# A transformer block on one core: feed-forward in two phases, attention beside recurrence, seven block products in place of eight

## The chip, the core and the metric

The kernel runs on one of the eight cores of one Trainium2 chip. The metric is the device time of one execution in microseconds. Five engines of the core work side by side, each with its own list of instructions, and wait for each other at semaphores: TensorE (PE, the matrix products; PEld is its loading of the stationary operand), VectorE (DVE), ScalarE (ACT), GpSimd (POOL) and SyncE (SP), which here only starts the transfers between device memory and on-chip memory. Products land in PSUM, eight banks of 128 x 512 f32; everything else in on-chip memory is SBUF.

## The reference

One block of an encoder is applied to two sequences with the same weights: S (`x_sample`, 512 tokens) and P (`x_prompt`, 1024 tokens), each with its own modulation. The width is 1024, the feed-forward width 2816 (22 tiles of 128).

```
mod = silu(c) @ w_mod + b_mod                 # sh1, sc1, gt1, sh2, sc2, gt2
h = rmsnorm(x, g_norm1) * (1 + sc1) + sh1
q, k, v, xr, gate = split(h @ w_in)           # 512, 128, 128, 512, 512 columns
attn = banded_attention(q, k, v, sink)        # window 128, 8 heads
lru = rglru_bidir(xr, ...) * gelu(gate)       # conv, gates, scan in both directions
mix = concat(rmsnorm(attn, g_attn_out), rmsnorm(lru, g_lru_out))
x = x + gt1 * (mix @ w_out)
h = rmsnorm(x, g_norm2) * (1 + sc2) + sh2
g_, u_ = split(h @ w_ffn_in)                  # 2816 columns each
x = x + gt2 * ((silu(g_) * u_) @ w_ffn_out)
y = rmsnorm(x, g_final)
```

## The kernel before

**Layout.** Activations lie transposed, features on the partitions and tokens in the free dimension, in chunks of 512 tokens: S is one chunk, P two. An f32 product is formed from three matmuls in a rounded format: each operand is split into a high and a low half (`split_on`, `Weights.high` and `low`: a rounding copy, `whi`, on ScalarE or sometimes VectorE, then a subtraction, `wlo`, on VectorE), and `mm3` issues high x high, high x low and low x high into one bank. A tile of output (128 features x 512 tokens) over 1024 inputs so takes 8 x 3 = 24 matmuls of 512 columns. The norms' sums over the partitions are matmuls of squared values (`sqt`, or split into `ssh` and `ssl`) with a matrix of ones, then a root and a reciprocal (`rstd`), with the result in `bc`.

**Order.** `program` (line 1190) runs the stages one after the other on TensorE: `start` (line 627: S's modulation and first norm), input products zS of S (14 tiles), zP of P (11 tiles; 2 tiles; 1 tile), with S's output product outS between the last two pieces, the feed-forward of S, the two output products outP of P, and the feed-forward of P. `W` (`Weights`, line 231) is the list of all weight tiles in the order of their use: each is loaded to one of N_WST staging tiles, split, used (`pop`) and given free.

**Main and side.** Everything that isn't a main product is a generator in `side` (line 289). `weave` runs the main stage step by step; after each step a side generator may take a step if the planner (`Plan`, a table of costs per engine) thinks its operands are ready, and no engine's backlog is too long. `side.finish(x)` issues all that is left of x at that place. The engines then run their lists as written; the planner only sets the order. All instructions carry line 85, where `Engine` calls the real engine, so groups are told apart by names.

**Around the change.** In S's feed-forward the side holds one chain (line 1264): P's attention, then P's recurrence, then the norm of mix (`mixnorm`, line 1015) of P's first chunk. The second chunk's `mixnorm` starts after `side.finish` of that chain. `ffn` (line 1061) alternates: two gate-and-up pairs (`unit_in`; `sg` is the gate's tile, `ach` and `acl` the split activation), then the output tiles of the two pairs (`unit_out`), whose eight banks are each drained into `x` on VectorE (`drain`), so that x collects the sum over eleven drains. The last of P's output is done in two halves of 256 tokens, each with its own final norm (`final`, line 1169). At line 1242 four chunks of modulation products (`mod_chunk`, line 495; `mst` are the loaded tiles, `mrow` the row) wait in the side from zS on, ahead of S's second norm.

Of the kernel before, what the change touches and what calls it, by code (L numbers as in the profile page):

```python
# [32 lines left out]
N_HEAP = 73  # L33
N_WHL = 10
N_WST = 3


def ffn_steps(chunks):


    every = tuple(range(chunks))
    steps = [("in", (j,), (c,)) for c in every for j in (0, 1)]
    for j in range(2, NFF - 2):
        steps.append(("in", (j,), every))
        if j >= 2 and j % 2 == 0:
            steps.append(("out", (j - 2, j - 1), every))
    last = (NFF - 2, NFF - 1)
    steps.append(("in", last[:1], every))
    for c in every:
        steps.append(("in", last[1:], (c,)))  # L50
        if c == 0:
            steps.append(("out", (NFF - 4, NFF - 3), every))
        steps.append(("out", last, (c,)))
    return steps


def ffn_tiles(step):
    kind, js, _ = step
    return [("f1", j + o) for j in js for o in (0, NFF)] if kind == "in" else [("f2", j) for j in js]
# [56 lines left out]
class Plan:  # L116
# [6 lines left out]
    def estimate(self, e, op, args, kw):  # L123
# [20 lines left out]
        elif e == "pool":  # L144
            cost = 0.1 + n / (930 if op in ("tensor_scalar", "memset") else 453) + 0.05 * columns
        else:
            cost, lag = n * outs[0].shape[0] * 4 / 360e3, 2.0
# [3 lines left out]
    def note(self, e, op, args, kw):  # L151
        if e == "dma":
            self.at["sp"] = max(self.at["sp"], self.done.get(kw["in_"].tensor.name, 0.0)) + 0.5
# [76 lines left out]

class Weights:


    def __init__(self, k, order):
        self.k, self.order = k, order
        self.n_load = self.n_hi = self.n_lo = self.n_pop = self.n_free = 0
        self.tiles = {}
        self.slots = [""] * N_WST

    def load(self, now=True):  # L240
        if self.n_load < len(self.order) and self.n_load - self.n_lo < N_WST:
            if not now and self.k.plan.used.get(self.slots[-N_WST], 0.0) > self.k.plan.at["pe"]:
                return
            self.k.plan.at["sp"] = max(self.k.plan.at["sp"], self.k.plan.used.get(self.slots[-N_WST], 0.0))
            t = self.k.wst.tile([P, 1024], F32, tag="wst", name="wst")
            self.k.sp.dma_start(out=t, in_=self.order[self.n_load][1])
            self.slots.append(t.tensor.name)
# [37 lines left out]
    def free(self, n=1):  # L285
        self.n_free += n
# [1083 lines left out]
```

## Time and profile before

| | us |
|---|---|
| median of 3 runs | 1746.13 (1744.09 to 1746.81) |
| profiled execution | 1742.62 |
| its span | 1740.8 |
| start and zS of S, to | 164 |
| zP, 13 tiles, to | 345.4 |
| outS, to | 391.5 |
| last z tile, S's second norm, to | 404.5 |
| feed-forward of S, P's attention and recurrence beside it, to | 867.5 |
| mix norms of P, to | 900.1 |
| outP, two chunks, to | 1002.3 |
| feed-forward of P, to | 1726.9 |
| last norm and output, to | 1740.8 |

The span is the profiled stretch from the first instruction to the last; the execution's own time is a little longer. The rows below come from the page of this execution and from views of its trace: windows, waits, groups of instructions by line and form, and the timeline. A weight's bank, tile or engine is named as in the code. The clock column is the TensorE clock that was granted as a share of 2.4 GHz. Matmuls overlap in the pipeline, so the mean of a group of them is longer than the time from one to the next; the latter is read from a count in a window.

### The profile page before, as it was taken

How to read it: one execution, taken by the hardware profiler on the slowest of the kernel's cores; microseconds unless marked ns; L12 is line 12 of the kernel's file. 1: busy time of each engine (PE TensorE's matmuls, PEld its weight loads, DVE VectorE, ACT ScalarE, POOL GpSimd, SP SyncE). 2: the span in 40 equal slices, each digit the busy share in tenths (PEclk: the TensorE clock that was granted, in tenths of full speed). 3: DMA queues.
4: the chain of work that ended last, by engine and by line, in shares of the span. 5: the costliest groups of instructions: out<-in, count | busy, mean ns of one | idle time of the engine just before them, and what ended most of it. 6: DMA issues, size and time to landing. Idle time of an engine off the chain costs nothing.

```text
span 1740.8 us, 19699 instructions
## 1 busy us (share of the span) xinstructions
PE 1651.2 (95%) x7428; PEld 1329.8 (76%) x7428; DVE 1058.5 (61%) x1733; ACT 694.9 (40%) x1135; POOL 95.7 (5%) x164
## 2 busy tenths in 40 slices
PE   7979999998999999999929999999999999999996
PEld 2656888786888887777717888888888888888885
DVE  5764876747887878787899754244244244244257
ACT  3343787525665555745735341111111111111114
POOL 0000111001222100000000000000000000000004
PEclk9988999999999999999959999999999999999999
DMA  8766322244222223233315311111111111111102
GB/s 304 266 249 212 109 91 97 86 144 158 96 63 84 73 91 127 85 115 108 104 37 188 118 46 49 49 49 49 49 49 49 49 49 49 49 49 49 49 0 97
DMA packets 70302, 166.84 MB, mean 96 GB/s; under 512 B 7360, under 2 KB 15808, under 8 KB 70208
## 3 DMA queue, kind: packets, MB, share of 16 engines
q1 hardware_dynamic: 70208, 165.59, 28.3%
q8 instruction: 58, 0.95, 0.2%
q14 instruction: 36, 0.29, 0.1%
HBM read 148.26 MB, written 17.30 MB: 95 GB/s over the span
## 4 chain that ended last, share of the span: by engine, by line
PE 82%; DVE 8%; ACT 4%; DMA 4%; issue 1%; SPq 0%; POOL 0%; POOLq 0%; DVEq 0%; ACTq 0%
PE pm L85 74%; PE ps L85 8%; DVE x L85 1%; DMA mst<-w_mod 1%; ACT ga L85 1%; DVE wlo L85 1%; DVE bc L85 1%; DVE lh L85 1%; DMA wst<-w_in 1%; ACT gs L85 1%; ACT gi L85 1%; DVE hl L85 1%; SPq L85 0%; DVE yo L85 0%; ACT whi L85 0%
## 5 line engine op out<-in xcount | busy, mean ns | idle before, releaser
L85 PE MATMUL pm<-hh,whi 128*128 128x512 f32 x1392 | 551.3, 396 | 1.6 <-ACT hh L85 1.3
L85 PE MATMUL pm<-hl,whi 128*128 128x512 f32 x1392 | 545.0, 391 | 3.5 <-DVE hl L85 3.5
L85 PE MATMUL pm<-hh,wlo 128*128 128x512 f32 x1392 | 544.9, 391 | 2.1 <-DVE wlo L85 2.1
L85 PEld LDWEIGHTS pm<-hh,whi 128*128 128x128 f32 x1392 | 263.1, 189 | 61.1 <-issue 5.8
L85 PEld LDWEIGHTS pm<-hh,wlo 128*128 128x128 f32 x1392 | 262.7, 189 | 58.4 <-DVE wlo L85 2.5
L85 PEld LDWEIGHTS pm<-hl,whi 128*128 128x128 f32 x1392 | 263.2, 189 | 56.9 <-DVE hl L85 4.4
L85 ACT ACTIVATE whi<-wst 128x1024 fp32r<-128x1024 f32 x164 | 168.5, 1051 | 294.1 <-issue 181.5
L85 DVE SCALAR_TENSOR_TENSOR x<-pm,modT,x 128x512 f32<-128x512 f32 (+1 forms) x296 | 212.7, 732 | 104.3 <-PE pm L85 103.6
L85 DVE TENSOR_TENSOR wlo<-wst,whi 128x1024 fp32r<-128x1024 f32 x184 | 223.3, 1228 | 9.4 <-ACT whi L85 8.1
L85 DVE TENSOR_TENSOR sg<-sg,pm 128x512 f32<-128x512 f32 x44 | 30.3, 688 | 321.6 <-PE pm L85 321.6
L85 PE MATMUL pm<-ach,whi 128*128 128x512 f32 (+1 forms) x544 | 211.7, 389 | 6.8 <-DVE x L85 4.8
L85 PE MATMUL pm<-acl,whi 128*128 128x512 f32 (+1 forms) x544 | 208.6, 383 | 0.3 <-DVE acl L85 0.3
L85 PE MATMUL pm<-ach,wlo 128*128 128x512 f32 (+1 forms) x544 | 208.5, 383 | 0.0
L85 ACT ACTIVATE ach<-sg 128x512 fp32r<-128x512 f32 x56 | 35.4, 632 | 270.9 <-DVE sg L85 270.9
L85 PEld LDWEIGHTS pm<-ach,whi 128*128 128x128 f32 x544 | 102.2, 188 | 34.8 <-DVE x L85 13.1
L85 PEld LDWEIGHTS pm<-ach,wlo 128*128 128x128 f32 x544 | 102.2, 188 | 20.3
L85 PEld LDWEIGHTS pm<-acl,whi 128*128 128x128 f32 x544 | 102.3, 188 | 19.4 <-DVE acl L85 0.5
L85 ACT ACTIVATE sg<-pm 128x512 f32<-128x512 f32 x66 | 39.4, 598 | 172.6 <-PE pm L85 172.6
L85 PE MATMUL pm<-mxh,whi 128*128 128x512 f32 x192 | 77.4, 403 | 12.0 <-ACT mxh L85 12.0
L85 PE MATMUL pm<-mxl,whi 128*128 128x512 f32 x192 | 77.0, 401 | 7.6 <-DVE mxl L85 7.6
L85 PE MATMUL pm<-mxh,wlo 128*128 128x512 f32 x192 | 76.1, 396 | 0.0
L85 POOL TENSOR_SCALAR sx<-sx,es 128x384 f32<-128x384 f32 (+1 forms) x96 | 60.0, 644 | 243.7 <-DVE es L85 132.0
(150 smaller groups left out, 1707.5 us busy)
## 6 DMA issues: line engine op xcount, KB each, us to landing
wst<-w_f SPq DMA_DIRECT2D x132, 512.0 KB, 3.6
mst<-w_mod SPq DMA_DIRECT2D x96, 256.0 KB, 5.4
wst<-w_in SPq DMA_DIRECT2D x28, 512.0 KB, 4.3
wst<-w_out SPq DMA_DIRECT2D x24, 512.0 KB, 3.7
x<-x_p SPq DMA_DIRECT2D x32, 256.0 KB, 4.7
x<-x_s SPq DMA_DIRECT2D x16, 256.0 KB, 4.5
y_p<-yo SPq DMA_DIRECT2D x16, 256.0 KB, 2.1
zq<-zo SPq DMA_DIRECT2D x12, 256.0 KB, 2.6
```

The lines of the kernel that those rows point to most:

```text
L85: r = fn(*args, **kw)
```

## The change

- **Seven for eight.** P's gate and up tiles are computed by a scheme of seven block products (`ffn_in_seven`). The weights of a pair are blocks of a 2 x 2 matrix by half of the inputs, the two chunks of P the other dimension. Products of sums of blocks take the place of the eight plain ones. The sums of the weights are formed per pair on VectorE (`Weights.group`: G, the gate's tile, S and D, sums and differences, U, one block); those of the activations once (`norm2_first`, `norm2_second`, `t1` to `t4`); the results are combined by additions from PSUM (`p`, `u`, `v`, `w`).
- **Two phases.** Gate and up tiles of all 22 pairs come first, and their activations go to device memory (`act_alloc`, `up`, `gated`); then the output product reads them back and splits them (`act_reader`), and stays in PSUM over all 22 tiles: `ffn_out_half` does four output tiles at a time in four banks (S), `ffn_out` all eight in eight banks (P, once per chunk, so that `w_f2` is loaded twice for P). S's second half is done after outP. The last piece of P is no longer cut in two.
- **Attention beside recurrence.** `lru` with its half of the mix norm (`mix_lru`) and `attention` with the other (`mix_att`) are two chains in the side, for both sequences.
- **Others.** `mod_chunk` issues each load from the third on once the load two before it is expected to have landed, instead of eight in a row; four of the modulation chunks enter the side ahead of the second piece of zP, and not with zS; z's cuts are 10 and 12 in place of 11 and 13; the residual `x` of the output products passes through device memory; staging tiles are 5, not 3; the planner's cost of transfers rises.

In the order of instructions this shows at three places. VectorE, in P's feed-forward, two weight tiles and a gate-and-up pair of both chunks, before:

```order
L85 TENSOR_TENSOR wlo<-wst,whi 128x1024 x2
L85 TENSOR_TENSOR sg<-sg,pm 128x512
L85 TENSOR_TENSOR acl<-sg,ach 128x512
L85 TENSOR_TENSOR sg<-sg,pm 128x512
L85 TENSOR_TENSOR acl<-sg,ach 128x512
```

and one pair of after (the weights' `ghi`, `shi` and their sums `wsum`, `wdif` stand between the combining additions):

```order
L61 TENSOR_TENSOR glo<-wst,ghi 128x1024
L61 TENSOR_TENSOR v<-u,pm 128x512
L61 TENSOR_TENSOR wsum<-wst 128x512
L61 TENSOR_TENSOR wsum<-wsum,wst 128x512
L61 TENSOR_TENSOR p_9190<-p_9190,pm 128x512
L61 TENSOR_TENSOR slo<-wsum,shi 128x1024
L61 TENSOR_TENSOR w<-u,pm 128x512
L61 TENSOR_TENSOR u<-v,pm 128x512
L61 TENSOR_TENSOR wdif<-wst 128x512
L61 TENSOR_TENSOR wdif<-wst,wsum 128x512
L61 TENSOR_TENSOR v<-v,ps 128x512
L61 TENSOR_TENSOR v<-v,p_9190 128x512
```

Before, a pair has two gate products and two low halves of activations (and two low halves of weights). After, it has seven additions from PSUM, and the sums and low halves of the weights stand in the same queue between them; the low half of an activation is no longer here.

VectorE at the end of the stage in which S's feed-forward runs; before, the last recurrence tile and the mix norm of P's first chunk (`lh`: recurrence, `ao`: attention):

```order
L85 TENSOR_TENSOR lh<-lh,gg 128x512 x2
L85 TENSOR_TENSOR sqt<-sqt 128x512 x5
L85 TENSOR_TENSOR ssl<-sqt,ssh 128x512 x2
L85 RECIPROCAL bc<-bc 128x128 x8
L85 SCALAR_TENSOR_TENSOR lh<-lh,vec,bc 128x512 x4
L85 SCALAR_TENSOR_TENSOR ao<-ao,vec,bc 128x512 x4
L85 TENSOR_TENSOR mxl<-lh,mxh 128x512 x4
L85 TENSOR_TENSOR mxl<-ao,mxh 128x512 x4
```

after, there are the drains of S's first half output (`x<-pm`) and the attention norm of P's second chunk, whose first chunk's came before them:

```order
L61 SCALAR_TENSOR_TENSOR x<-pm,modT,x 128x512
L61 SCALAR_TENSOR_TENSOR ao<-ao,vec,bc 128x512 x4
L61 SCALAR_TENSOR_TENSOR x<-pm,modT,x 128x512 x2
L61 TENSOR_TENSOR sqt<-sqt 128x512 x2
L61 SCALAR_TENSOR_TENSOR x<-pm,modT,x 128x512
L61 TENSOR_TENSOR sqt<-sqt 128x512
L61 CAST mxh<-ao 128x512
L61 TENSOR_TENSOR mxl<-ao,mxh 128x512 x4
L61 TENSOR_TENSOR sqt<-sqt 128x512 x3
L61 TENSOR_TENSOR ssl<-sqt,ssh 128x512
```

What stood behind the whole of attention and recurrence is now the end of one chain, behind four drains.

SP, a quarter into zS, before (`mst`: modulation tiles, `zk`, `zq`: z's pieces to memory, `wst`: weights):

```order
L85 DMA sel_84<-sel 2x2 x4
L85 DMA x<-x_p 128x512 x8
L85 DMA zk_0_115<-zo 128x512
L85 DMA wst<-w_in 128x1024
L85 DMA zq_0_114<-zo 128x512
L85 DMA wst<-w_in 128x1024
L85 DMA mst<-w_mod 128x512 x16
```

and after:

```order
L61 DMA sel_84<-sel 2x2 x4
L61 DMA wst<-w_in 128x1024 x2
L61 DMA x<-x_p 128x512 x8
L61 DMA zk_0_114<-zo 128x512
L61 DMA wst<-w_in 128x1024
L61 DMA zq_0_113<-zo 128x512
L61 DMA wst<-w_in 128x1024
L61 DMA mst<-w_mod 128x512 x3
```

The sixteen loads in a row are gone; three stand there, and the weight tiles that came behind them follow at once.

The diff, cut to its core:

```diff
-N_HEAP = 73
+N_HEAP = 72
-N_WST = 3
+N_WST = 5
...
+    def group(self, gate, up):
+        half = slice(0, CH), slice(CH, 2 * CH)
+        def gen(it):
+            yield self.may_stage(it),
+            g = self.fetch(it, gate)
+            yield self.may_stage(it),
+            u = self.fetch(it, up)
+            tt = self.k.dve.tensor_tensor
+            g0, g1, u0, u1 = (t[:, h] for t in (g, u) for h in half)
+            G = yield from self.split(it, g, "g")
+            yield self.may_stage(it), u
+            t = self.stage(it, "wsum")
+            s1, s2 = (t[:, h] for h in half)
+            tt(out=s1, in0=u0, in1=u1, op=ALU.add)
+            yield ()
+            tt(out=s2, in0=s1, in1=g0, op=ALU.subtract)
+            S = yield from self.split(it, t, "s")
+            yield self.may_stage(it),
+            d = self.stage(it, "wdif")
+            d3, d4 = (d[:, h] for h in half)
+            tt(out=d3, in0=g0, in1=u0, op=ALU.subtract)
+            yield ()
+            tt(out=d4, in0=g1, in1=s2, op=ALU.subtract)
...
+            D = yield from self.split(it, d, "d")
...
+            yield self.may_split(it, 1),
+            U = self.slot(it, "u")
+            self.k.cpy.copy(out=U[:, half[0]], in_=u1)
+            yield U,
+            tt(out=U[:, half[1]], in0=u1, in1=f(U)[:, half[0]], op=ALU.subtract)
...
+            it.out = G, S, D, U
...
             ws.append(t)
+            if k > 1:
+                yield ws[k - 2],
...
+    def norm2_second(self, seq, R0, R, ops):
...
+            t3 = self.T("t3")
+            sub(t3, b22, b12)
+            yield ()
+            sub(b12, b12, b11)
+            ops["22"][i] = yield from self.split_on(b22, "b")
+            sub(b22, b22, b12)
+            yield b22,
+            ops["t2"][i] = yield from self.split_on(b22, "t")
+            sub(b21, b21, b22)
...
+    def ffn_in_seven(self, W, ops, acts, ahead):
+        def product(w, o, key):
+            if self.seven % 8 < 4:
+                ps, free = self.pm(), self.pm_done
+            else:
+                ps = self.ps()
+                free = lambda: self.shut(ps)
...
+            for i in range(4):
...
+                self.mm3(ps, wh[:, at], (wh if wl is None else wl)[:, al], xh, xl, i == 0, i == 3)
...
+        for j in range(NFF):
...
+            G, S, D, U = W.pop(("g", j))
+            d = {"n": 0}
+            soon(first(d, *(yield from product(G, 0, "11"))))
+            soon(sums(d, 1, *(yield from product(S, 1, "t2")), ("u", "p")))
+            soon(sums(d, 2, *(yield from product(D, 0, "t3")), ("v", "u")))
+            soon(sums(d, 3, *(yield from product(G, 1, "21")), ("p", "p")))
+            W.free(*G)
+            soon(sums(d, 4, *(yield from product(S, 0, "t1")), ("w", "u"), ("u", "v")))
+            W.free(*S)
+            soon(gated(d, 6, *(yield from product((U, None), 0, "t4")), [("v", "v")], "p", "v", acts[0][j]))
+            W.free(U)
+            soon(gated(d, 7, *(yield from product(D, 1, "22")), [("w", "w")], "w", "u", acts[1][j]))
+            W.free(*D)
...
+    def act_reader(self, acts, ahead):
+        got = {}
+        def fetch(j):
+            t = self.T("ac")
+            self.sp.dma_start(out=t, in_=acts[j])
+            def cut():
+                yield t,
+                got[j] = yield from self.split_on(t, "ac")
+            self.side.soon(cut())
...
+    def ffn_out(self, seq, R, W, get, late, end, ahead, done):
...
+        def share(j, m):
+            if j == 0:
+                ps[m] = self.pm() if m < 4 else self.ps()
+            sl = slice(m * P, (m + 1) * P)
+            self.mm3(ps[m], ws[j][0][:, sl], ws[j][1][:, sl], *av[j], j == 0, j == NFF - 1)
...
-        CUT1, CUT = 11, 13
+        CUT1, CUT = 10, 12
...
-        side.finish(s_lru, s_att)
-        s_mix = side.add(self.mixnorm(0, AOs, Ls, SQs, mixS))
+        s_mod2 = side.add(mods(6, 7, 8, 9))
...
-        s_mix = side.add(chain(self.attention(1, 2, zP, AOp), self.lru(1, 2, zP, Lp, SQp),
-                               self.mixnorm(0, AOp, Lp, SQp, mixP[0])))
+        s_lru = side.add(chain(self.lru(1, 2, zP, Lp, SQp), *(self.mix_lru(c, Lp, SQp, mixP[c]) for c in range(2))))
+        s_att = side.add(chain(self.attention(1, 2, zP, AOp), *(self.mix_att(c, AOp, mixP[c]) for c in range(2))))
...
+        side.weave(self.ffn_in([RS], W, False, actS, lambda: reads.append(self.act_reader(actS[0], 4))))
...
+        side.weave(self.ffn_out_half(0, RS, W, reads.pop(), 0, accS))
+        side.finish(s_lru, s_att)
         side.weave(out_main(1, 0, mixP[0], RP[0]))
...
+        s_norm = side.add(self.norm2_first(1, RP[0], ops))
...
         side.weave(out_main(1, 1, mixP[1], RP[1]))
...
+        s_norm2 = side.add(self.norm2_second(1, RP[0], RP[1], ops))
+        side.weave(self.ffn_out_half(0, RS, W, reads.pop(), 1, accS))
...
+        side.finish(s_norm, s_norm2)
+        side.weave(self.ffn_in_seven(W, ops, actP, read(0)))
+        ops.clear()
+        for c in range(2):
+            side.weave(self.ffn_out(1, RP[c], W, reads.pop(0), 2 * c, c == 1, read(1) if c == 0 else lambda: None, done_p(c)))
```

## Rows read from the trace of the kernel before

**Rows 1.** The page: busy time of two engines, GB/s by slice, weight loads' landing.
```profile
PE 1651.2 (95%) x7428; PEld 1329.8 (76%) x7428; DVE 1058.5 (61%) x1733; ACT 694.9 (40%) x1135; POOL 95.7 (5%) x164
...
GB/s 304 266 249 212 109 91 97 86 144 158 96 63 84 73 91 127 85 115 108 104 37 188 118 46 49 49 49 49 49 49 49 49 49 49 49 49 49 49 0 97
...
wst<-w_f SPq DMA_DIRECT2D x132, 512.0 KB, 3.6
```

**Rows 2.** Windows: stretch, busy PE, PEld, DVE, ACT, POOL, clock, DMA share, GB/s.
```profile
35.00:165.00 130.00, 114.02 (x516) 82.72 (x516) 82.85 (x145) 50.90 (x75) 0.00 (x0) 0.91 0.66 236
345.40:391.50 46.10, 43.98 (x193) 35.73 (x193) 23.26 (x29) 14.13 (x18) 0.00 (x0) 1.00 0.43 143
391.50:404.50 13.00, 11.74 (x52) 9.37 (x50) 9.12 (x12) 7.30 (x10) 1.42 (x4) 1.00 0.19 62
404.50:415.00 10.50, 7.44 (x24) 5.58 (x24) 9.47 (x15) 5.35 (x9) 0.00 (x0) 0.84 0.94 300
404.50:867.50 463.00, 451.71 (x2127) 369.07 (x2128) 373.52 (x697) 277.61 (x490) 44.75 (x80) 1.00 0.32 102
867.50:900.10 32.60, 2.84 (x6) 1.07 (x4) 30.03 (x42) 12.24 (x21) 0.00 (x0) 0.58 0.08 26
900.10:1002.30 102.20, 95.23 (x392) 76.44 (x393) 87.04 (x115) 45.29 (x64) 3.16 (x2) 0.93 0.42 142
905.00:910.00 5.00, 5.00 (x11) 3.26 (x10) 3.46 (x6) 0.69 (x2) 0.00 (x0) 0.50 0.19 39
1002.30:1726.90 724.60, 723.61 (x3228) 599.36 (x3226) 288.02 (x373) 139.88 (x192) 10.55 (x10) 1.00 0.14 46
1100.00:1150.00 50.00, 50.00 (x222) 41.40 (x221) 17.96 (x23) 8.12 (x11) 0.00 (x0) 1.00 0.13 42
1726.90:1740.80 13.90, 1.58 (x7) 1.06 (x6) 9.98 (x13) 4.08 (x10) 8.55 (x11) 0.73 0.44 151
```

**Rows 3.** Waits of PE, 840 to 1000 us: total, times, longest.
```profile
PE ps L85 <- ACT ssh L85: 18.8, 1, 18.8
PE pm L85 <- ACT mxh L85: 12.0, 2, 10.5
PE pm L85 <- DVE mxl L85: 5.5, 3, 3.5
```

**Rows 4.** Groups by line and form, whole span: busy us, mean ns, idle before.
```profile
L85 DVE TENSOR_TENSOR wlo<-wst,whi 128x1024 fp32r<-128x1024 f32 x184 | 223.3, 1228 | 9.4 <-ACT whi L85 8.1
L85 DVE SCALAR_TENSOR_TENSOR x<-pm,modT,x 128x512 f32<-128x512 f32 x280 | 205.8, 747 | 102.5 <-PE pm L85 101.8 <-issue 0.5
L85 DVE TENSOR_TENSOR sqt<-sqt 128x512 f32<-128x512 f32 x67 | 46.0, 687 | 8.9 <-ACT sqt L85 6.4
L85 DVE TENSOR_TENSOR acl<-sg,ach 128x512 fp32r<-128x512 f32 x66 | 45.8, 694 | 31.3 <-ACT ach L85 30.8
L85 DVE TENSOR_TENSOR sg<-sg,pm 128x512 f32<-128x512 f32 x44 | 30.3, 688 | 321.6 <-PE pm L85 321.6
L85 DVE SCALAR_TENSOR_TENSOR x<-x,A,bc 128x512 f32<-128x512 f32 x16 | 11.4, 746 | 0.0
L85 DVE RECIPROCAL bc<-bc 128x128 f32<-128x128 f32 x56 | 47.6, 909 | 19.0 <-ACT bc L85 19.0
L85 DVE SCALAR_TENSOR_TENSOR yo<-x,vec,bc 128x512 f32<-128x512 f32 x12 | 10.2, 882 | 0.0
L85 ACT ACTIVATE whi<-wst 128x1024 fp32r<-128x1024 f32 x164 | 168.5, 1051 | 294.1 <-issue 181.5 <-PE pm L85 93.5 <-DMA wst<-w_in 15.6
L85 ACT ACTIVATE sqt<-x 128x512 f32<-128x512 f32 x63 | 38.2, 627 | 33.7 <-DVE x L85 29.3 <-DMA x<-x_s 3.6 <-DMA x<-x_p 0.5
L85 ACT ACTIVATE mxh<-ao 128x512 fp32r<-128x512 f32 x12 | 7.2, 622 | 1.7 <-DVE ao L85 1.6
L85 ACT ACTIVATE sqt<-ao 128x512 f32<-128x512 f32 x12 | 6.6, 616 | 0.0
L85 ACT ACTIVATE sg<-pm 128x512 f32<-128x512 f32 x66 | 39.4, 598 | 172.6 <-PE pm L85 172.6
L85 ACT ACTIVATE bc<-ps,eps 128x512 f32<-128x512 f32 x14 | 9.5, 686 | 13.8 <-PE ps L85 13.8
```

**Rows 5.** Timeline: start, us, engine, operation (the squares' matmuls, the last output).
```profile
1705.25 1.02 PE L85 MATMUL ps<-sqt,ones_d 128*128 128x512 f32 x2
...
1734.07 3.52 POOL L85 TENSOR_TENSOR yo<-x,bc 128x256 f32<-128x256 f32 x4 [1.26 <-DVE bc L85]
```

**Rows 6.** Waits, 85 to 97 us: total, times, longest.
```profile
PE ps L85 <- ACT mrow L85: 7.4, 1, 7.4
ACT whi L85 <- DMA wst<-w_in: 6.4, 1, 6.4
```

More of the change, by code (lines that the diff above doesn't have):

```diff
@@ L381, in ps @@
     def ps(self):
+        while not self.plan.banks:
+            if self.side.fast:
+                self.side.urge(1)
+            else:
+                self.side.step(min(self.side.gens, key=lambda g: self.plan.when(g[1])))
         self.plan.banks.pop(0)
@@ L1049, in out_drain @@
         self.pm_done()
+        yield x,
+        self.sp.dma_start(out=R["dram"][m], in_=x)
         yield from self.square_on(x, R["acc"])
@@ new lines, in act_alloc, with gate @@
+    def act_alloc(self, seq, C):
+        return [[self.dram.tile([P, CH], F32, name=f"ac{seq}_{c}_{j}", tag=f"ac{seq}_{c}_{j}") for j in range(NFF)]
+                for c in range(C)]
+    def gate(self, ps, d, native):
+        yield ps,
+        s = d["s"] = self.T("sg")
+        if native:
+            self.act.activation(out=s, in_=ps, func=AF.Silu)
+        else:
+            self.act.activation(out=s, in_=ps, func=AF.Tanh, scale=0.5)
+            yield s,
+            self.dve.scalar_tensor_tensor(out=s, in0=s, scalar=1.0, in1=ps, op0=ALU.add, op1=ALU.mult)
+        self.pm_done()
+        d["gate"] = True
@@ new lines, in act_reader, with get @@
+    def act_reader(self, acts, ahead):
[7 more added lines that the diff above has]
+            self.side.soon(cut())
+        for j in range(ahead):
+            fetch(j)
+        def get(j):
+            if j + ahead < len(acts):
+                fetch(j + ahead)
+            while j not in got:
+                self.side.urge(1)
+            return got.pop(j)
+        return get
@@ new lines, in ffn_out, with take, drop @@
+    def ffn_out(self, seq, R, W, get, late, end, ahead, done):
+        ps, ws, av = [None] * KT, {}, {}
+        x = R["x"] = [None] * KT
+        gate = self.modT[:, seq, 40:48]
+        cut = NFF - 2
+        def share(j, m):
[3 more added lines that the diff above has]
+            self.mm3(ps[m], ws[j][0][:, sl], ws[j][1][:, sl], *av[j], j == 0, j == NFF - 1)
+        def take(j):
+            ws[j], av[j] = W.pop(("f2", j)), get(j)
+        def drop(j):
+            W.free(*ws.pop(j))
+            del av[j]
+        for j in range(cut):
+            take(j)
+            if j == NFF - 4:
+                ahead()
+            if j == NFF - 5:
+                for m in range(KT):
+                    x[m] = self.T("x")
+                    self.sp.dma_start(out=x[m], in_=R["dram"][m])
+            for m in range(KT - 1):
+                share(j, m)
+                if m % 2:
+                    yield
+            if j >= late:
+                share(j - late, KT - 1)
+                drop(j - late)
+            yield
+        S = []
+        for j in range(cut, NFF):
+            take(j)
+        for m in range(KT):
+            for j in range(cut - late if m == KT - 1 else cut, NFF):
+                share(j, m)
+            self.side.soon(self.down(ps[m], x[m], m, gate, S, end, self.pm_done if m < 4 else lambda m=m: self.shut(ps[m])))
+            yield
+        for j in range(cut - late, NFF):
+            drop(j)
+        self.side.urge(len(self.side.fast))
+        done(slice(0, CH), S)
```

467 lines of the change are left out of this document (268 added, 199 removed).

## The prediction

> **What bounds the kernel now.** I read the page first: TensorE is busy 95% of the span, VectorE 61% [rows 1], so in most stretches a shorter TensorE stream is a shorter kernel. Then I cut the span into its stages by windows [rows 2]. In the second sequence's feed-forward (1002.3 to 1726.9) TensorE is busy 723.61 of 724.60 us and VectorE only 288; a 50 us stretch of it holds 222 matmuls of 512 columns, that is 0.2252 us each. It is the only stage with nothing left to fill. Elsewhere TensorE loses time in four places. At the end of the first sequence's feed-forward (867.5 to 900.1) it is busy 2.84 of 32.6 us; the waits there are one of 18.8 us for ssh and two of 12.0 for mxh, the mix norm of the second sequence [rows 3]. After that idleness the granted clock is at the lower level, 1.2 GHz: 11 matmuls in 5 us, 0.45 us each, the clock column at 0.50 [rows 2]. Near the start (35 to 165) TensorE is busy 114 of 130 us at a mean clock of 0.91. At 391.5 to 415 it waits for the first sequence's second norm. After the last matmul 13.9 us follow.
>
> **Seven products for eight.** Before, 22 pairs of gate and up tiles x 2 x 2 chunks x 24 = 2112 matmuls; after, 22 x 7 x 12 = 1848. The 264 that go are worth 264 x 0.2252 = 59.5 us, all on the path. What pays is VectorE and ScalarE. VectorE per pair, by the nearest rows [rows 4]: three low halves of 1024 columns (1.228 each, 3.7), four block sums and one low half of 512 (0.687, 3.4), seven additions from PSUM (0.688, 4.8), two gate products (0.69, 1.4): 13.3 us against 84 x 0.2252 = 18.9 us of TensorE. ScalarE: 3 x 1.051, one 512 cast, one copy and two Silu of some 0.6: 5.6 us. Both hide. The weights' preparation is a chain (cast, low half, sums, cast, low half, sums, cast, low half, cast, low half: some 11 us), and G, S and D of the next pair need buffers that this pair's products release, so it starts beside the pair and not before it. Its last piece, D, starts when the fifth product ends, at 13.5 us, is ready some 3 us later, and is used in the third product of the next pair: covered. If the cover fails, the pair is late by what sticks out (a rival below); if TensorE runs dry here at all, I know no row that shows it: between 0 and that rival's price I take 3 us.
>
> **Two phases.** The output matmuls keep their number (1056, and 528 for the first sequence) and now stay in PSUM over all 22 tiles instead of going into x every second tile. 88 of VectorE's drains of 0.747 us go in the first sequence and 160 in the second. The second sequence loads its 22 output tiles twice, and activations pass through memory: one 512 KB and one 256 KB transfer per 24 matmuls, 5.4 us, about 145 GB/s. The page's first slice shows 304 [rows 1], VectorE has 1.23 + 0.69 of 5.4 us to do. I cost this at nothing; a phase whose first tile isn't fetched early waits for one landing, 3.6 us [rows 1], and there are four phases, so 0 to 14. The halved last pieces (96 matmuls of 256 columns) become 48 of 512: the stage takes 724.6 where 3168 x 0.2252 = 713.4 would do, so 0 to 11 us; I take 3.
>
> **The end.** With no halves, the last chunk's norm is one piece. After the last matmul: eight f32 matmuls over the squares at up to 1.02 (8.2), root 0.7, four reciprocals of 0.909 (3.6), six outputs of 0.882 (5.3), and the 3.2 us that lie between the last output piece and the end now [rows 4, 5]: 21 us against 13.9, so +7 (bounds +3, if the squares' matmuls overlap the last drain, and +9).
>
> **Attention beside recurrence.** Window 404.5 to 867.5: VectorE 373.5 busy, plus 30.0 in the hole after it. From 403.5 go 88 drains (65.7) and 11 weight tiles now later (13.5), and about 10 for the second chunk's norm come in: 334 us, against TensorE's 463 - 11.3 idle - 59.5 moved = 392. So VectorE no longer limits, and the two chains that ran one behind the other (attention, then recurrence, then norm) have 392 us for the longer one. What remains at the end of the stage is seen in the order of instructions: the second chunk's attention norm stands behind the four drains of the half output phase. From the last matmul: drain 0.75, square 0.63, three casts of 0.62, four squares of 0.62 [rows 4], an add, a cast and a low half 2.0, waits between them: 8.5 us idle, then about 10 us at half clock, 5 more. Before, from 867.5: 29.8 idle, and in the next stage, which has 384 matmuls and 8 small ones (2.5), 102.2 - 86.5 - 2.5 = 13.2, together 43 [rows 2]. After, with 1.5 for small waits, 15: gain 28 (bounds 0 and 36).
>
> **The first sequence's second norm** is now covered by two z tiles (21.6 us) instead of one (10.8). At 391.5 to 404.5 TensorE idles 1.3 us, at 404.5 to 415 3.1 us at clock 0.84: gain 5 (0 to 6).
>
> **The start.** The SP queue issues sixteen w_mod loads in a row ahead of a w_in tile; ScalarE then waits 6.4 us for that tile with the modulation row behind it, and TensorE 7.4 for the row [rows 6]. The change loads three at a time and moves four of the six chunks to the stage at 345.4, where the transfer engines are busy 0.43 and not 0.66 of the time. Lost now [rows 2]: 16 us idle, and, as a mean of 0.91 between 1.00 and 0.50 means, 0.18 of 130 us at the lower level, about 8 more where TensorE worked. Their matmuls are only moved. I take 13 back (0 to 22), because VectorE was 64% busy there and the norms it carries don't shrink.
>
> **The hand-over to the seven products.** The half output phase (264 matmuls, 59.5 us) covers the second norm with its differences and splits. In the new order VectorE has, from the second chunk's last drain to what the second product needs, 8 low halves of 1024 (9.8), 18 of activations (12.5), 15 differences (10.3), 18 splits (12.4), 4 block sums (2.7), 8 scalings (6.0) and 4 reciprocals (3.6): 57 us [rows 4], a tie. I take +4 (0 to +14), and +2 for other seams. With the 3 of the seven products this is +9.
>
> Sum on the profiled execution (1742.62: its 1740.8 span and 1.8 around it): -59.5 - 3 + 7 - 28 - 5 - 13 + 9 = -92.5, so 1650. The median of the runs stands 3.5 above that execution, within their own scatter; I don't add it.
>
> A rule of the skill against this. The second sequence's output phase goes round eight PSUM banks with three matmuls in each; the present one goes round four with six, and shows a granted clock of 1.00 in all of its 724.6 us [rows 2]. The Trainium skill, "TensorE: Matmul & The Clock Gate", section "A second HAM failure mode: psum-queue depth-cycling", says that a kernel which cycled through its banks each iteration idled a little between groups, and its clock swung between the two levels. By the trace the sum is 1650; what the rule would make of it is the fourth rival. The present stage doesn't bear the rule out for four banks, and no row shows eight.
>
> **Rivals.** *The stall stays* (0.17): attention and recurrence share VectorE's queue and ScalarE's, and neither ends earlier than today. For it: in the hole VectorE is busy 30.0 of 32.6 us. Against: 79 us of its work leave the stage. Price 28: 1678. *The weights' chain sticks out* (0.11) by 2 us per pair, since casts and low halves stand in one queue behind sums that wait for products: 22 x 2 = 44, 1694. Against: 5 us of slack per pair by the count above. *More is gained* (0.12): the start gives back all 22 us, the hand-over is clean and the hole is halved again: 1650 - 9 - 9 - 7 = 1625. *The clock falls in the output phases* (0.04), the slower side: if TensorE idles between banks and is granted 1.2 GHz, each of 1584 matmuls costs 0.45 in place of 0.225. All of them: 1650 + 363 = 2013; it decides from 96 / 0.229 = 420 matmuls, about a quarter, and at a half of them the time is 1830. *It doesn't do what it says* (0.03): the pairs run at the pace of eight products, because psum release by VectorE sets the pace, and the hole stays: 1650 + 59.5 + 28 = 1738.
>
> **Numbers.** Forecast 1650 with 0.53, its own range 1636 to 1666. Less than 0.2% (3.5 us) can't be told from no change here. Faster: 0.53 + 0.17 + 0.11 + 0.12, most of 0.03, less a little for mishaps together: 0.93; within 0.2%: 0.02; slower: 0.05. The range 1614 to 1698 leaves out the clock rival, the last one and the sums of several bad ends.
>
> **What would show it.** The stage of seven products: 416 us for 1848 matmuls, 222 per 50 us, clock 1.00, VectorE near 70%. Two output stages of 119 us each. At the end of the first half output phase one wait of TensorE for ssh or ssl of 6 to 11 us. In 35 to 165 no ScalarE wait above 3 us for a w_in tile. About 21 us after the last matmul. I am wrong if the seven products take over 430 us, if the hole is over 20 us, or if the clock falls in an output stage.

## The result, and the profile after

The changed kernel takes 1637.09 us (median of 4 runs, 1636.23 to 1637.56) against 1745.11 of the kernel before in the same series: a ratio of 0.9382, with a 95% interval of 0.9365 to 0.9398. Forecast were 1650 us, in a range of 1614 to 1698. All medians here are of the usual executions: one execution of one kernel below ran from 30 us on at a mean granted clock of 0.55, took 2694.5 us and is left out. The page of the changed kernel, whose span is 1635.3 us: the rows that answer to [rows 1].

```profile
PE 1581.5 (97%) x7120; PEld 1273.0 (78%) x7120; DVE 1148.4 (70%) x1846; ACT 793.4 (49%) x1257; POOL 98.6 (6%) x148
...
GB/s 336 226 255 145 97 91 135 166 253 180 168 114 112 123 116 104 127 150 127 114 230 190 133 127 112 78 77 85 90 88 86 78 78 210 134 184 156 185 148 52
...
wst<-w_f SPq DMA_DIRECT2D x154, 512.0 KB, 3.7
```

TensorE has 308 recorded matmuls less and 69.7 us less of busy time, and VectorE and ScalarE have more to do. Windows of the changed kernel, with the columns of [rows 2], one row per stage (the stretch from 165.0 to 368.8 is left out): the start; the two z tiles with S's second norm; S's gate and up tiles with the last of the modulation; the first output half; the hole; P's output product; the second output half; the seven products; a stretch of 50 us in them; P's output; the end.

```profile
35.00:165.00 130.00, 123.13 (x556) 94.79 (x556) 102.62 (x182) 73.92 (x112) 2.40 (x7) 0.99 0.61 210
368.80:391.00 22.20, 22.20 (x99) 18.34 (x99) 17.82 (x24) 12.68 (x17) 0.00 (x0) 1.00 0.28 96
391.00:711.00 320.00, 313.01 (x1496) 256.66 (x1495) 270.46 (x498) 233.38 (x404) 44.24 (x64) 0.99 0.40 131
711.00:789.80 78.80, 77.38 (x377) 64.68 (x376) 67.27 (x142) 45.41 (x94) 15.97 (x20) 1.00 0.48 155
789.80:803.70 13.90, 1.55 (x4) 0.81 (x4) 11.49 (x19) 6.19 (x12) 0.00 (x0) 0.62 0.29 105
803.70:892.60 88.90, 88.90 (x387) 73.44 (x386) 62.80 (x81) 41.38 (x58) 0.00 (x0) 0.98 0.57 186
892.60:953.00 60.40, 60.40 (x268) 49.79 (x266) 56.52 (x81) 38.57 (x59) 0.00 (x0) 1.00 0.46 153
953.20:1373.40 420.20, 419.98 (x1850) 347.29 (x1851) 290.49 (x393) 127.38 (x165) 2.75 (x2) 1.00 0.29 94
1100.00:1150.00 50.00, 50.00 (x223) 41.39 (x222) 34.82 (x47) 14.95 (x20) 0.00 (x0) 1.00 0.28 87
1373.40:1613.70 240.30, 240.30 (x1060) 198.66 (x1059) 101.90 (x118) 78.49 (x99) 3.43 (x2) 1.00 0.47 153
1613.70:1635.30 21.60, 7.07 (x17) 2.85 (x16) 10.21 (x11) 2.54 (x4) 3.44 (x2) 0.78 0.25 97
```

The reader is to see three things. In the seven products TensorE is idle for 0.2 of 420.2 us, at a clock of 1.00, with VectorE at 69%. The largest hole left is 13.9 us, where 32.6 stood [rows 2]. The end is longer, 21.6 for 13.9.

Stage by stage, by the windows of the two traces; where 48 matmuls moved from one stage to another, they are set right at 0.2252 us each:

| stage | forecast | measured | from |
|---|---|---|---|
| P's feed-forward | -59.5 - 3 + 3 | -64.1 | 724.6 to 660.5 |
| hole and P's output product | -28 | -32.0 | 134.8 to 102.8 |
| start to the end of outS | -13 | -11.9 | 391.5 to 368.8, with 48 matmuls (10.8) less |
| S's norm and feed-forward, hand-over | -5 + 6 | -5.2 | 476.0 to 421.0 + 60.6, with 48 matmuls more |
| end | +7 | +7.7 | 13.9 to 21.6 |
| sum | -92.5 | -105.5 | 1740.8 to 1635.3 |

### The profile page after: what moved, and what is told of

It reads as the page before. It is cut to its first block, busy times and chain, and to the rows that moved or that the text cites. A ratio compares the mean times of both kernels' runs of the same rounds, so it can differ in the third digit from the quotient of the medians.

```text
span 1635.3 us, 19943 instructions
## 1 busy us (share of the span) xinstructions
PE 1581.5 (97%) x7120; PEld 1273.0 (78%) x7120; DVE 1148.4 (70%) x1846; ACT 793.4 (49%) x1257; POOL 98.6 (6%) x148
## 4 chain that ended last, share of the span: by engine, by line
PE 82%; ACT 7%; DVE 6%; DMA 2%; issue 2%; SPq 0%; DVEq 0%; ACTq 0%
PE pm L61 54%; PE ps L61 28%; ACT ga L61 2%; ACT gi L61 1%; ACT gs L61 1%; DMA mst<-w_mod 1%; DVE lh L61 1%; DVE bc L61 1%; DVE hl L61 1%; DVE x L61 1%; DVE wlo L61 0%; ACT L61 0%; SPq L61 0%; DVE ao L61 0%; DMA qf<-zq 0%
## 5 line engine op out<-in xcount | busy, mean ns | idle before, releaser
L61 PE MATMUL pm<-hh,whi 128*128 128x512 f32 x688 | 275.8, 401 | 0.2 <-DVE hh L61 0.2
L61 PE MATMUL pm<-hh,wlo 128*128 128x512 f32 x688 | 270.5, 393 | 2.1 <-DVE wlo L61 2.1
L61 PE MATMUL pm<-hl,whi 128*128 128x512 f32 x688 | 270.6, 393 | 0.5 <-DVE hl L61 0.5
L61 PEld LDWEIGHTS pm<-hh,whi 128*128 128x128 f32 x688 | 130.6, 190 | 30.9 <-issue 4.4
L61 PEld LDWEIGHTS pm<-hh,wlo 128*128 128x128 f32 x688 | 130.3, 189 | 30.7 <-DVE wlo L61 2.5
L61 PEld LDWEIGHTS pm<-hl,whi 128*128 128x128 f32 x688 | 130.4, 190 | 25.9 <-DVE hl L61 1.1
L61 PE MATMUL pm<-ach,whi 128*128 128x512 f32 x352 | 138.3, 393 | 1.4 <-DVE sg L61 1.4
L61 PE MATMUL pm<-ach,wlo 128*128 128x512 f32 x352 | 137.1, 390 | 0.0
L61 PE MATMUL pm<-acl,whi 128*128 128x512 f32 x352 | 137.1, 390 | 0.0
L61 PEld LDWEIGHTS pm<-acl,whi 128*128 128x128 f32 x352 | 66.1, 188 | 13.3 <-issue 0.2
L61 PE MATMUL ps<-acl,whi 128*128 128x512 f32 x176 | 68.5, 389 | 0.0
```

The costliest lines, as they stand in the source:

```text
L61: r = fn(*args, **kw)
```

## The experiments

Eleven kernels, each the changed one with an edit, are compared with its 1637.09 us.

**Eight products in two phases.** Only the scheme of P's gate and up tiles goes back to eight plain products, with a second norm that needs no sums and differences; phases, chains and loads stay as changed.

```diff
-        W.order += [(("g", j), W.group(a["w_f1"][j], a["w_f1"][NFF + j])) for j in range(NFF)]
-        W.order += [(key, W.plain(ap)) for key, ap in f2 + f2]
+        W.order += [(key, W.plain(ap)) for key, ap in f1_order + f2 + f2]
...
-        side.weave(self.ffn_in_seven(W, ops, actP, read(0)))
+        side.weave(self.ffn_in(RP, W, True, actP, read(0)))
...
```

> The two-phase kernel with P's gate and up tiles by eight plain products again. Theory (the 264 matmuls are all on TensorE's path and nothing else pays): +59.5 us on 1637, the stage of gate and up 476 us, so 1695 to 1700. Rival (release of the banks by VectorE, or the chain of the weights, sets the pace of the seven products): the stage is shorter by less than 59.5 us with seven, so under 1690. Rival 2 (the second norm with its differences costs time at the hand-over): eight products need no differences and win some of it back, 1685 to 1693.

Measured: 1694.6 us (1694.2 to 1698.4), +57.5; ratio to before 0.9724 (0.971 to 0.9739). That is just under the theory's 1695 and above the 1693 of its second rival, so the price is read from the stage itself. The windows of this kernel, gate and up tiles and then P's output:

```profile
955.10:1434.70 479.60, 479.60 (x2115) 396.75 (x2115) 113.57 (x128) 60.52 (x80) 3.37 (x2) 1.00 0.24 79
1434.70:1675.00 240.30, 240.30 (x1059) 198.60 (x1059) 100.31 (x115) 78.34 (x98) 3.75 (x2) 1.00 0.44 148
```

Eight products take 479.6 us and seven 420.2: 59.4 less, the full price of 264 matmuls, while VectorE goes from 113.6 to 290.5. Both go at the same pace, 0.227 us per matmul. And the two phases with whole pieces at the end take 719.9 us where before took 724.6 with the same work: 4.7 us come from the phases and the whole pieces together, not from the scheme.

**VectorE loaded on purpose.** In the groups of the seven products the three low halves of 1024 columns are computed twice, and three times.

```diff
-        self.k.dve.tensor_tensor(out=lo, in0=src, in1=f(hi), op=ALU.subtract)
+        for _ in range(1 if name == "w" else 2):      # 3 in the second kernel
+            self.k.dve.tensor_tensor(out=lo, in0=src, in1=f(hi), op=ALU.subtract)
```

> Each low half of the groups' G, S and D is computed twice: 3 x 1.23 = 3.7 us more of VectorE per pair of the seven products. Theory (VectorE has 13.2 of 19.1 us to do, and the chain of the weights has time to spare): no change, 1635 to 1642. Rival (the chain of the weights is just in time, each delay of it sticks out): 22 x 2 to 3.7 = 44 to 81 us slower.

> The same low halves three times: 7.4 us more per pair. Theory: VectorE has 20.6 us per pair against 18.9 of TensorE, so it sets the pace and the stage takes 22 x 20.6 = 453 us and more: +33 to +50, 1670 to 1690. Rival (the chain just in time): +100 and more. If there is no change, the slack is larger than the busy time says.

Measured: 1644.4 us (+7.3) and 1689.4 us (+52.3). From the start of its first matmul to that of its last, the stage of seven products goes from 419.8 to 426.6 and 468.8 us. Windows of the stage in the first and in the second of these kernels, and the second's longest waits of TensorE there:

```profile
953.00:1379.60 426.60, 422.28 (x1849) 347.80 (x1850) 363.29 (x459) 127.00 (x168) 2.87 (x2) 1.00 0.29 92
```

```profile
957.30:1426.00 468.70, 432.30 (x1849) 348.32 (x1850) 437.22 (x523) 124.81 (x169) 3.48 (x2) 0.99 0.26 84
```

```profile
PE pm L61 <- DVE dlo L61: 16.0, 10, 3.0
PE ps L61 <- DVE dlo L61: 15.6, 11, 1.6
```

From the first matmul of a pair to that of the next the trace has, for the first pairs and then each of the rest:

| kernel | 1st | 2nd | 3rd | from the 5th on |
|---|---|---|---|---|
| as changed | 20.08 | 19.19 | 19.04 | 19.04 |
| low halves twice | 24.78 | 19.04 | 21.29 | 19.04 |
| three times | 24.90 | 24.87 | 24.53 | 20.7 to 20.8 |

With 3.7 us more the first and the third pair pay, beside the rest of the second norm, and no later one. They make up 6.8 of the 7.3 us; the expected 1635 to 1642 left them out. With 7.4 each pair waits once for the low half of D, and takes 20.8 us. VectorE's queue sets the pace then; the stretch around that wait in one pair of the second kernel:

```profile
1094.62 0.68 DVE L61 TENSOR_TENSOR v<-v,pm 128x512 f32<-128x512 f32 x1
1095.22 0.68 DVE L61 TENSOR_TENSOR wdif<-wst 128x512 f32<-128x512 f32 x1
1095.82 0.69 DVE L61 TENSOR_TENSOR wdif<-wst,wsum 128x512 f32<-128x512 f32 x1
1097.69 3.74 DVE L61 TENSOR_TENSOR dlo<-wdif,dhi 128x1024 fp32r<-128x1024 f32 x3 [1.19 <-ACT dhi L61]
```

That the count said 20.6 is in part luck: additions that stand back to back follow each other at 0.60 us and not at 0.69, and in each pair VectorE stands 1.2 us for ScalarE's cast of D, a step of the chain that the count of busy time doesn't hold. The room per pair lies between 3.7 us, which cost a late pair nothing, and 5.7 (7.4 less the 1.7 that a pair became longer); the busy times said 5.6. The rival with a chain that is just in time falls.

**One chain.** P's attention, recurrence and the four mix norms stand in one chain.

```diff
-        s_lru = side.add(chain(self.lru(1, 2, zP, Lp, SQp), *(self.mix_lru(c, Lp, SQp, mixP[c]) for c in range(2))))
-        s_att = side.add(chain(self.attention(1, 2, zP, AOp), *(self.mix_att(c, AOp, mixP[c]) for c in range(2))))
+        s_att = s_lru = side.add(chain(self.attention(1, 2, zP, AOp), self.lru(1, 2, zP, Lp, SQp),
+                                       *(g for c in range(2) for g in (self.mix_lru(c, Lp, SQp, mixP[c]),
+                                                                       self.mix_att(c, AOp, mixP[c])))))
...
```

> P's attention, recurrence and the four mix norms stand in one chain again, all else as changed. Theory (two chains side by side are what shrank the hole in front of the output product): the hole grows from 14 us to some 30 to 45, 1653 to 1668. Rival (the hole shrank because VectorE lost its drains and splits, in whatever order): within 5 us of 1637.

Measured: 1691.5 us, +54.4: the theory's direction, and far more than its 16 to 31. A window and the waits of TensorE in this kernel:

```profile
775.60:856.90 81.30, 13.10 (x27) 6.05 (x27) 53.48 (x75) 45.51 (x69) 0.00 (x0) 0.53 0.07 23
```

```profile
PE ps L61 <- ACT ssh L61: 57.6, 4, 24.9
PE ps L61 <- ACT gi L61: 9.5, 4, 6.7
```

The chain isn't done when the 1320 matmuls beside it end: the last tile of the recurrence fills the first half of the hole (to 817 us in the trace, where the wait of 24.9 for ssh ends), and the four norms follow one after the other (four waits for ssh). VectorE is busy 53.5 of 81.3 us: what the chain waits for is mostly its own steps, each on the last. The second chain isn't free, either: with one, the 1320 matmuls take 408.5 us and with two 420.8; the hole is 67 us longer. The hole of before was smaller since it held two of the four norms, and all 1584 matmuls stood ahead of it.

**Both output halves ahead of P's output product.**

```diff
...
         side.weave(self.ffn_out_half(0, RS, W, reads.pop(), 0, accS))
+        reads.append(self.act_reader(actS[0], 4))
+        side.weave(self.ffn_out_half(0, RS, W, reads.pop(), 1, accS))
         side.finish(s_lru, s_att)
...
-        reads.append(self.act_reader(actS[0], 4))
...
-        side.weave(self.ffn_out_half(0, RS, W, reads.pop(), 1, accS))
```

> S's second output half stands beside the first, ahead of P's output product, and no longer covers P's second norm. Theory (the 60 us of that half hide the second norm, its differences and splits, some 57 us of VectorE): the hole in front of P's output goes (-14), but TensorE is idle some 30 to 45 us ahead of the second of the seven products, and then a while at the lower clock: 1655 to 1675. Rival (the norm keeps pace with the first pairs' products by itself): 1623 to 1630.

Measured: 1660.65 us (1659.81 to 1661.05), +23.6. A further execution, for its trace:

> The same kernel as in the run with both output halves of S ahead of P's output product, for a profile. Theory: no idle time of TensorE ahead of P's output product; after that product one stretch of 25 to 35 us in which it waits, the longest wait for a low or high half of t2 or of the second chunk's norm, and a lower clock behind it. Rival: the 24 us are spread over the first pairs of the seven products, whose weights' chain is late.

Measured: 1661.02 us. Its windows around P's output product and the start of the seven products, and the waits of TensorE there:

```profile
859.00:946.60 87.60, 87.60 (x388) 72.43 (x386) 59.27 (x78) 37.12 (x51) 0.00 (x0) 1.00 0.48 159
946.60:995.00 48.40, 26.09 (x79) 17.84 (x78) 43.73 (x65) 23.31 (x37) 0.00 (x0) 0.68 0.02 6
```

```profile
PE pm L61 <- ACT th L61: 14.1, 2, 7.8
PE pm L61 <- DVE tl L61: 5.1, 4, 1.8
PE ps L61 <- ACT ssh L61: 2.9, 1, 2.9
```

The hole is gone (0.2 us from one matmul to the next at 859), and the second norm with its differences now lies open: TensorE idles 22.3 of 48.4 us, above all for halves of the differences (`th`, `tl`), and the clock falls. The seven products with the way to them take 30 us more. A further 7 us are lost at 790, where the second half waits for activations that nobody fetched early (one wait of 6.6 for ach), and 1 elsewhere. -14 + 8 + 30 = +24.

**One chain and both halves**, the order of before in these two points.

> One chain for P's attention, recurrence and norms, and both output halves of S ahead of P's output product: the order of the kernel before in these two points, with the drains and splits of the new one. With one chain alone the hole was 81 us; with both halves alone there was none and the kernel took 24 us more than as changed. Theory (one chain is too long by some 80 us for the 1320 matmuls beside it, and 264 more cover 60 of that): a hole of 20 to 30 us, 1675 to 1692. Rival (with both halves ahead the order of the chains is worth nothing): 1658 to 1665.

Measured: 1688.0 us (1687.5 to 1688.2), +50.9. A window of the hole and the waits of TensorE in it:

```profile
852.20:884.20 32.00, 4.82 (x8) 1.93 (x7) 26.22 (x39) 12.65 (x21) 0.00 (x0) 0.56 0.15 48
```

```profile
PE ps L61 <- ACT ssh L61: 26.2, 3, 12.3
```

Beside the same 1584 matmuls two chains leave no hole and one leaves 32 us; the second chain is worth 27 us here (1688 - 1661). This hole is as long as that of before, but holds three norms, those of the second chunk too, which before stood beside the first chunk's output product. So the single chain gets further than before's beside as many matmuls. That fits the relief of VectorE, which wasn't tried alone, and it isn't enough.

**Half of the norm later.** Only the first chunk's attention norm is finished ahead of P's output product.

```diff
-        s_att = side.add(chain(self.attention(1, 2, zP, AOp), *(self.mix_att(c, AOp, mixP[c]) for c in range(2))))
+        s_att = side.add(chain(self.attention(1, 2, zP, AOp), self.mix_att(0, AOp, mixP[0])))
...
         side.finish(s_lru, s_att)
+        s_att = side.add(self.mix_att(1, AOp, mixP[1]))
         side.weave(out_main(1, 0, mixP[0], RP[0]))
+        side.finish(s_att)
```

> Only the first chunk's attention norm is finished ahead of P's output product; the second chunk's is left to run beside the first chunk's product. Theory (what remains of the hole is the second chunk's norm, which the first product doesn't need): the hole falls from 14 to 5 to 8 us, 1629 to 1632. Rival (the first chunk's split stands behind the drains and lands at 799, so little goes): 1633 to 1637. Rival 2 (the norm now delays the drains of the first product): no gain or slower.

Measured: 1631.87 us (1631.35 to 1632.68), -5.2: ratio to before 0.936 (0.9345 to 0.9376). The gap from one matmul to the next is 6.9 us instead of 14.1, and the product behind it takes 91.2 instead of 88.8. The wait that is left:

```profile
PE pm L61 <- ACT mxh L61: 6.6, 1, 6.6
```

It is for the first chunk's attention. So half of the hole was the second chunk's norm, and half was not.

**The start**, three kernels: loads not paced; chunks 6 to 9 back with zS; both.

```diff
-            if k > 1:                                     # first and third kernel
-                yield ws[k - 2],
...
-        s_mod = side.add(mods(4, 5))                      # second and third
+        s_mod, s_mod2 = side.add(mods(4, 5)), side.add(mods(6, 7, 8, 9))
...
-        s_mod2 = side.add(mods(6, 7, 8, 9))
```

> The modulation loads come eight in a row again; chunks 6 to 9 stay at the later place, all else as changed. Theory (the pacing keeps the weight tiles from standing behind the loads): the stretch 35 to 165 loses 5 to 8 us again, and some more near 300 us where the four chunks now run: 1642 to 1650. Rival (the later place or the two more staging tiles brought the start's gain): within 3 us of 1637.

> The four modulation chunks 6 to 9 enter the side with zS again, but paced, all else as changed. Theory (both parts share the gain of 12 us): 4 to 8 us slower, 1641 to 1645. Rival (pacing alone suffices): within 3 us of 1637.

> Chunks 6 to 9 enter the side with zS and are loaded eight at a time, as in the kernel before; all else as changed. With them early and paced the kernel took 20 us more than as changed, with them late and not paced 7 more. Theory (the place decides, because the four chunks compete with P's first norm for VectorE, ScalarE and the transfers; pacing is worth little): 1652 to 1665. Rival (pacing spreads the early chunks out so that they hold back the norm; unpaced they would be over sooner): 1640 to 1650.

| | as changed | not paced | early | early, not paced |
|---|---|---|---|---|
| median | 1637.1 | 1644.4 | 1657.5 | 1664.8 |
| end of outS in the trace | 368.6 | 370.4 | 389.8 | 393.0 |

The place is worth 20.4 us with either way of loading, the pacing 7.3 or 7.4 with either place. They add up, so neither carries the other. Two of the theories missed a size: early chunks were expected to cost 4 to 8 us, and pacing to be worth little beside them. A third met the time and not the place. Without pacing, with the chunks late, 35 to 165 was to lose 5 to 8 us, and it loses nothing:

```profile
35.00:165.00 130.00, 124.06 (x560) 96.17 (x560) 101.43 (x176) 72.38 (x106) 2.35 (x7) 0.99 0.62 212
```

The traced execution of that kernel is 4.9 us longer than that of the changed one. Some 2 of them lie at the end of outS and 4 in front of P's output product, where the hole is 18.1 us and not 14.1. Windows of the kernel with both undone, and its two longest waits of TensorE from 35 to 350 us:

```profile
35.00:165.00 130.00, 112.48 (x503) 81.44 (x503) 82.40 (x145) 51.37 (x75) 0.00 (x0) 0.89 0.70 243
165.00:345.00 180.00, 172.21 (x817) 142.16 (x815) 135.78 (x279) 129.22 (x235) 26.80 (x46) 0.99 0.32 104
345.00:395.00 50.00, 48.84 (x200) 39.80 (x201) 23.18 (x29) 15.93 (x20) 0.00 (x0) 0.92 0.46 147
```

```profile
PE ps L61 <- ACT mrow L61: 14.8, 2, 8.4
PE pm L61 <- ACT mxh L61: 6.0, 1, 6.0
```

The stretch 35 to 165 is that of before [rows 2] (114.0 busy, clock 0.91), with the wait for the modulation row [rows 6] twice. So the two edits are the whole of the gain there. But with both undone outS ends at 393.0, and in the kernel before it ends at 391.5 with 10.8 us more of z tiles done: something else in the change costs some 12 us at the start. Of these, 4 lie in the z tiles, 6 are the wait for S's mix norm in front of outS, and 2 lie in outS behind it, 48.0 us with a clock of 0.92 for 46.0 at 1.00 [rows 2].

**Three edits together**, meant to beat both kernels: the later norm as above; the first four tiles of P's output product begin with the recurrence's inputs; and at the end the first six squares are added on VectorE.

```diff
...
-        if apart or not S:
+        if apart and m > 5 or not S:
             S.append(t)
...
+        def out_split(seq, c, mix, R):
...
+                self.out_part(*held[m], mix, range(4, KT), True)
...
+            for m, (w, ps) in enumerate(held):
+                self.out_part(w, ps, mix, range(4), False)
+                self.side.soon(self.out_drain(seq, m, R, ps))
...
```

> Three edits on the changed kernel: the second chunk's attention norm runs beside the first chunk's output product (alone: 5.2 us less); the first four tiles of that product begin with the recurrence's half of the inputs, which is ready earlier than attention's; and at the end the first six squares are added on VectorE, so that three matmuls over squares stand at the end and not eight. Theory (what is left of the hole is attention's norm of the first chunk, 7 us, with a while at the lower clock behind it; and the tail waits for 16 passes over squares of 0.44 us, 7.0 us, of which ten go): 8 to 10 us from the hole and 3.5 to 4.5 from the tail below 1632, so 1617 to 1621. Rival (the adds delay the last drains, or the norm still ends late): 1624 to 1632.

Measured: 1618.56 us (1617.76 to 1619.29), ratio to before 0.9274 (0.926 to 0.9287), 18.5 less than the changed kernel. Its windows where the hole was, there with P's output product, and at the end:

```profile
789.80:803.70 13.90, 13.90 (x63) 11.35 (x62) 12.05 (x19) 6.71 (x13) 0.00 (x0) 1.00 0.53 186
789.80:878.00 88.20, 88.20 (x390) 72.82 (x389) 73.75 (x101) 46.57 (x69) 0.00 (x0) 1.00 0.62 205
1599.20:1616.90 17.70, 2.97 (x7) 0.83 (x6) 10.59 (x12) 3.17 (x5) 3.44 (x2) 0.67 0.31 119
```

The hole is filled, -14.7 us with its slower matmuls (the later norm alone brought 5.2; the second and the third edit weren't tried alone), and from the last product to the end it takes 18.0 us where 21.8 stood.

## Why the prediction was right, and where its sum was off

The direction and the two large terms hold, and none of the three signs of being wrong was seen. The sum was 13 us short, nearly all of it at three terms that were sized on the careful side: the hand-over, the hole and P's feed-forward.

**The seven products**: forecast 416 us, 222 matmuls per 50 us, clock 1.00 and VectorE near 70%; measured 420.2, 223, 1.00 and 69%. Some 3 of the 4 us are a matter of reading: 222 in 50 us counts matmuls that the window's edges cut. From start to start the trace has 0.2267 us, in both kernels, and not 0.2252; so the 264 are worth 59.9 us. VectorE's 13.3 us per pair, summed from rows of other operations [rows 4], are measured as 13.3 (34.82 of 50 us, at 19.04 per pair). The 3 us taken for dry spells aren't there, but for 1 in the first pair: seven and eight products go at one pace. The rival of the weights' chain falls with the two loaded kernels.

**The halved pieces** were under-sized: 3 us of 0 to 11 were taken, 4.7 measured, together with the phases, by the kernel with eight products; at 0.2267 us a matmul the bound is 6 and not 11. The phases themselves were costed at nothing, and from stage to stage the changed kernel has 0.2 us between matmuls; the landing that was feared shows only where nothing was fetched early (6.6 us, with both output halves ahead).

**The hole**: forecast 28, measured 32. One wait for ssh of 12.4 us stands there, a little over the 6 to 11 that were named. The reason given, the second chunk's norm behind four drains, is half of it: with that norm later, 6.9 of 14.1 us stay, a wait for the first chunk's. The waits of TensorE from 700 to 1000 us in the changed kernel, to be read against [rows 3]:

```profile
PE ps L61 <- ACT ssh L61: 12.4, 1, 12.4
PE pm L61 <- DVE sg L61: 1.4, 1, 1.4
PE pm L61 <- DVE x L61: 0.2, 1, 0.2
```

But the 5 us at half clock behind it weren't to be seen: the product behind the hole has a mean clock of 0.98, some 2 us. The step that began with VectorE's relief (373.5 us and 30.0 before, 334 forecast, 349 in the three windows from 391.0 to 803.7) left open what the second chain adds. The kernel with one chain and both halves has the relief and still a hole of 32 us with three norms in it; the second chain is what removes it. So the rival in which the stall stays falls. The hole that is left with two chains comes from the half of the output product that was moved behind.

**The hand-over** was the largest miss: the allowance of +4, and +2 for other seams, was taken for a tie of 57 us of VectorE's work against 59.5 us of TensorE's; measured 0.6 us between the last matmul of one and the first of the other. The work is there (VectorE is busy 56.5 of 60.4 us) and was counted rightly. It fits, as the rival with more gain had it: the same norm without the cover costs 30 us, nearly all of them in the first pair, which takes 46.4 us and not 20.1.

**The start** came out at the right size, 11.9 for 13, by luck: the sum was wrong in its parts. The sign that was named is there: in 35 to 165 the trace has no wait of ScalarE for a w_in tile. But up to the end of outS the two edits are worth 24, not 13, and another part of the change, which the sum had at nothing, costs 12. What that part is wasn't settled. 8 of the 12 are the wait for S's mix norm and the slower outS behind it; the z cut one tile earlier, with 10.8 us less of cover for S's attention and recurrence, would fit that. It wasn't tried alone, and neither were the five staging tiles, the residual's way through memory and the planner's new costs.

**The end**: +7 forecast, +7.7 measured. The timeline of the changed kernel after the last product, to be read against [rows 5]:

```profile
1620.81 0.69 ACT L61 ACTIVATE bc<-ps,eps 128x512 f32<-128x512 f32 x1 [5.45 <-PE ps L61]
1621.39 1.32 ACT L61 ACTIVATE x<-x,vec 128x512 f32<-128x512 f32 x2
1621.53 3.39 DVE L61 RECIPROCAL bc<-bc 128x128 f32<-128x128 f32 x4 [6.83 <-ACT bc L61]
1624.95 6.07 DVE L61 SCALAR_TENSOR_TENSOR yo<-x,vec,bc 128x512 f32<-128x512 f32 x6
1625.05 3.44 POOL L61 TENSOR_TENSOR yo<-x,bc 128x512 f32<-128x512 f32 x2 [107.14 <-DVE bc L61]
```

From the last product (1613.52) to the root are 7.3 us of matmuls over squares where 8.2 were counted, the six outputs take 6.07 where 5.3 were, and behind them 4.3 us follow where 3.2 were; the misses nearly cancel.

**The clock rival** didn't happen: P's output, which goes round eight banks with three matmuls in each, shows 1.00 in all its 240.3 us, and its matmuls follow each other at 0.227 us, with no idle time between banks. (The kernel before goes round four banks for its eight output tiles.) The Trainium skill, "TensorE: Matmul & The Clock Gate", section "A second HAM failure mode: psum-queue depth-cycling", tells of a kernel that idled a little between its groups of matmuls as it went through the banks. The trace doesn't agree for this loop, since it doesn't idle between its groups; what such idling would cost no run here shows.

## What to carry to other kernels

A scheme that trades matmuls for additions paid in full here, where TensorE had no gaps and VectorE's work per group, summed from rows, stayed well under TensorE's time (13.3 of 19.0 us); load the other engine on purpose to learn how much room is left. One stretch of main work can't cover two chains: with S's second output half moved ahead, the hole in front of P's output went, and twice as much was lost where that half had covered the second norm. What helped was to leave the piece that the next product doesn't need until that product runs, and, in the kernel with three edits, to begin the product with the inputs that are ready. When two edits are judged by one stage's lost time, undo each alone: their worth can be larger than the loss that was seen, since another edit spends a part of it.

## What was not expected of the hardware

The place of 8 MB of modulation weights is worth 20 us, although nothing of the work changes. With them early, TensorE's idle time from 35 to 392 us grows from 10.4 to 21.2 us, as seven windows sum up, and what the clock column lacks to 1.00 grows, weighed by the same windows, from 5.6 to 16.0 us. The two together give the 21.2 us by which outS ends later; by this estimate half of the price is not the waiting, but the lower clock that goes with it. The two windows in which it shows most, in the changed kernel:

```profile
100.00:135.00 35.00, 33.95 (x166) 24.83 (x164) 26.31 (x37) 19.88 (x28) 0.00 (x0) 1.00 0.75 253
...
300.00:345.00 45.00, 43.44 (x191) 34.48 (x192) 23.43 (x33) 18.04 (x24) 0.00 (x0) 0.92 0.70 239
```

and with chunks 6 to 9 early and paced:

```profile
100.00:135.00 35.00, 32.22 (x149) 23.01 (x151) 24.26 (x37) 18.06 (x26) 0.00 (x0) 0.85 0.64 236
...
300.00:345.00 45.00, 34.85 (x147) 27.69 (x145) 33.73 (x58) 23.44 (x37) 4.56 (x4) 0.89 0.23 81
```

The matmuls over f32 squares at the end go as 16 passes in 7.03 us, 0.44 us each. The last six outputs on VectorE take 1.01 us each beside GpSimd's two, and took 0.882 as a mean over the kernel before [rows 4].
